# Two transformer blocks on one core: a merge placed later, a staging buffer moved, expert choice in pieces, and narrow second blocks in the 64-expert mixture

## The chip, the cores and the metric

The kernel runs on one core of a Trainium2 chip. The time is the device time of one execution in microseconds (us); less is better. Several executions are timed and their median is taken. One execution of the kernel before was recorded by the hardware profiler, and all rows below come from that one.

## What is computed

Two blocks follow each other on x of 1024 rows by 1024 numbers (float32). Of the reference only the parts that the change touches are shown:

```python
# first block, end of its attention: 16 heads of 64 columns each (yb), and a gated merge with a recurrence (ya)
merged = gates[:, :, 0] * ya + gates[:, :, 1] * yb
h = h + merged @ w_out            # then a mixture of 32 experts, 2 for each row
# second block
mix = concatenate([o, p])         # o: gated recurrence of 4 heads, p: pooling, each through its small products
h = layer_norm(ALPHA * h + mix @ w_out_2)
scores = sigmoid(h @ w_router)    # 64 experts, 8 groups of 8
# 4 best groups by the sum of their 2 best, in them the 8 best experts; their weights normed and scaled
routed[row] += weight * ((silu(h[row] @ w_gate[e]) * (h[row] @ w_up[e])) @ w_down[e])   # 8 experts e per row
out = layer_norm(ALPHA * h + routed + shared_expert(h))
```

w_gate and w_up of an expert are 1024x256, w_down is 256x1024: 3 MB in float32.

## The kernel before, in words

**Attention** (L834 ff., about 728 to 1093 us). One stream of products runs on PE over the 16 heads; a head has eight key tiles, kt 0 to 7. `beside(h, kt)` (L1067) names the work that is put beside head h at tile kt: pieces of the next head's inputs, `rec` (L975), which fetches the finished pair's rows of the recurrence's output into one tile (bufs=1) on SP, and the six parts of `merge` (L986) for a finished pair of heads pr. `MERGE` (L832) lists for each part the head from which it is due and the tile. Parts 0 and 1 multiply the attention's rows, 2 and 3 add the gated recurrence on DVE, 4 copies the rounded half to `mgh` on ACT (L999, two copies), 5 forms the remainder `mgl` on DVE (L1002, two instructions), releases the pair's buffers and sends the loads of the next pair's gates on SP (`gates`, L1009). Parts 3 and 4 both stand at kt=1, part 5 at kt=2. On the same ACT the scores of each key tile are turned to exponentials (L950), and PE's score products (L947 to L949) wait for the score buffers that these free.

**The second block's mixer** (`mixer2`, L2048). SBUF pools are stacks: a pool that is opened where another was closed waits for the readers of that memory. `mixer2` opens the pool `hc` (with `v`, the recurrence's rows) first and `hw` (weights of its input product) behind it. At its end the 4x128x128 weights of the pooling are loaded and split in tiles of `hw`; then `back` (transposes of `v` on PE, L2353) and `pool` alternate. `mixer_out2` (L2366) is next: w_out_2 comes in eight pieces of 512 KB over SP (L2388) into tiles `s0` to `s2` of a shared pool `sh`, which lie where `v` was; each piece is split by ACT (L247) and DVE (L253).

**mixer_out2's loop** goes over eight tiles t of 128 rows, in two halves of 512 columns: 48 products of 256 columns on PE, the residual on DVE (L2461), then `norm(t)` (DVE, ACT, POOL), and behind it for tile t-2 `trans` (PE, copies on ACT L2429) in half 0 and `router` (PE L2435, ACT) in half 1. At `router(3)`, in t=5, half 1, the choice of experts for the first four tiles, `route2` (L2469), is issued in one stretch: an activation on ACT and some 65 DVE instructions. The other four tiles' `route2` is issued later, in pieces, inside the mixture.

**The mixture of 64 experts** (`moe2`, L2578, and `experts`, L1382; about 2121 to 3134 us). The experts are ranked by load; rank r has room for `CAPS2[r]` rows (L2576), and a program path for overflows lies behind it. The blocks of at most 128 rows come in pairs of experts: rank 63-i whole (128 rows), rank i as 128 rows and a second block with the rest of its room. So with `CAPS2` of before pairs 0 to 3 have a second block of 96 rows, pairs 4 to 31 one of 64. The rank-i expert's weights are split in two roundings and its first block uses three products each (`mm3`, L271 to L273); the whole expert's block and the 64-row second block use plain float32 products, each of which the trace records as two. A 64-row block (`half`, L1477) puts its output on two parts of the PE columns: rows of x stand still as 64 columns, and two products with halves of the weights run on the column parts 0 and 64 (`products2`, L1481, `tile_position`).

For each block n, in this order: gather of n+3 (POOL, indirect DMA, L1569), `gate_up`, `act`, `down(n-1)` and its scatter-add, `trans(n+2)`, `h_trans(n)`, and what `todo` holds for n: one-hots (DVE) and `tabmm` (PE, L1504), which make the index tables that the gathers and scatters read, each group of blocks due four blocks ahead. The scatter-add of a block (L1691 for 128 rows, L1666 for a 64-row one) is an indirect DMA from POOL that adds to `acc_d` in DRAM; as each writes the same tensor, each waits until the one before has landed. `y`, the block's result, has two buffers, `xg`, the gathered rows, three. Weights come in thirds of 1 MB through a ring of `RAW2`=11 (L1953), and `pump` (L1425) sends the next one over SP when PE has freed its place.

Of the kernel before, what the change touches and what calls it, by code (L numbers as in the profile page):

```python
# [7 lines left out]
F32 = mybir.dt.float32  # L8
# [12 lines left out]
D = 1024  # L21
# [210 lines left out]
class Body:  # L232
# [599 lines left out]
    MERGE = (2, 0), (3, 0), (3, 0), (3, 1), (3, 1), (3, 2)  # L832

    def attention(self, rb, rk, ml):  # L834
# [4 lines left out]
        with ExitStack() as cx:  # L839
# [227 lines left out]
            def beside(h, kt):  # L1067
# [5 lines left out]
                if n < 16:  # L1073
                    if kt < 2:
                        fill += [(t_piece, n, "kq"[kt], half) for half in range(2)]
                    fill += [(m_piece, n, i, a) for i, a in
                             {3: [(7, 0), (7, 512), (6, 0)], 4: [(6, 512), (5, 0), (5, 512)],
                              5: [(4, 0), (4, 512), (3, 0)], 6: [(2, 0), (1, 0), (0, 0)]}.get(kt, ())]
                    if kt == 5:
                        fill.append((v_piece, n))  # L1080
                    if kt == 7:
                        fill += [(lambda: None,), (row_piece, n)]
                if kt == (3 if h == 15 else 4) and h > 0:
# [3 lines left out]
                for part, (late, at) in enumerate(self.MERGE):  # L1087
                    if h >= late and (h - late) % 2 == 0 and kt == at:
                        fill.append((merge, (h - late) // 2, part, 0, 2, nc.vector if part else nc.gpsimd))
# [292 lines left out]
    def experts(self, cx, blocks, xsrc, wsrc, acc_d, C, route, pre=None, fin=None, whole=lambda key: False):  # L1382
# [9 lines left out]
        N = len(blocks)  # L1392
        n0 = next(n for n, b in enumerate(blocks) if b[0] is not None)
# [8 lines left out]
        split_to = {b[2]: n for n, b in enumerate(blocks) if b[0] is None or b[3] != 64}  # L1402
# [74 lines left out]
        def half(n):  # L1477

            return blocks[n][0] is not None and blocks[n][3] == 64
# [10 lines left out]
        def onehot(n, oh=None):  # L1490
            r, off = blocks[n][:2]
            oh = ohs[n] = ep.tile([128, 8, C], BF, name="oh") if oh is None else oh
            W = 64 if half(n) else C
# [3 lines left out]
        def tabmm(n, first, a=0, b=6):  # L1497
# [3 lines left out]
            for t in range(8):  # L1501
                for h in range(2 if half(n) else 1):
                    p, kw = (slice(64 * h, 64 * h + 64), dict(tile_position=(0, 64 * h))) if half(n) else (slice(C), {})
# [4 lines left out]
        def tabfin(first, size, a=0, b=6):  # L1508
# [19 lines left out]
            for j in range(size):  # L1528
                R = blocks[first + j][3]
                idx[first + j] = (gi[:R, j:j + 1], si[:R, j:j + 1],  # L1530
                                  w[:, j:j + 1] if half(first + j) else w[:R, j:j + 1], w)
# [5 lines left out]
        while first < N1:  # L1537
            size = min((3, 2, 2, 4, 8)[min(i, 4)] if n0 else (2, 3, 4, 6, 8)[min(i, 4)], N1 - first)
            last = n0 - 2 + 2 * i if n0 and i < 2 else first - 3 if not n0 and i == 2 else \
                first - 4 if n0 or i > 2 else i - 2  # L1540
# [20 lines left out]
        def gather(n):  # L1561
# [3 lines left out]
            xg = ep.tile([128, D], F32, name="xg", bufs=3)  # L1565
# [7 lines left out]
        def trans(n):  # L1573
# [9 lines left out]
            if whole(blocks[n][2]) or half(n):  # L1583
# [11 lines left out]
        def gate_up(n, mid=None):  # L1595
            key, R = blocks[n][2:]
            ps = pg.tile([128, 512], F32, name="gups")
            if half(n):
                j = 3 * keys.index(key)
                products2(ps[:, 0:256], X.pop(n), [lambda h, w=w: w[:, :, 128 * h:128 * h + 128]  # L1600
                                                   for w in gu([raw[j], raw[j + 1]])])
# [15 lines left out]
        def act(n):  # L1617
# [3 lines left out]
            R, W = (128, 128) if half(n) else (R, 256)  # L1621
# [5 lines left out]
        def h_trans(n):  # L1627
            hh, R = Hs[n], blocks[n][3]
            ps = p1.tile([128, 2, C], F32, name="hT")
            if half(n):  # L1630
# [3 lines left out]
                ps = ps.rearrange("p (k c) -> p k c", k=2)  # L1634
            else:
# [3 lines left out]
            if whole(blocks[n][2]) or half(n):  # L1639
# [10 lines left out]
        def down(n):  # L1650
# [5 lines left out]
            if half(n):  # L1656
                ps = p1.tile([128, 1024], F32, name="yps")[:, 0:512]
                j = 3 * keys.index(key) + 2
                products2(ps, h, [lambda q, w=w: w[:, q * 512:q * 512 + 512] for w in down_(raw[j])])
                if last_of[key] == n:  # L1660
# [3 lines left out]
                nc.scalar.activation(y[:64, 0:512], ps[:64], AF.Copy, scale=w[:64])  # L1664
                nc.vector.tensor_scalar(y[:64, 512:1024], ps[64:128], w[64:128], None, op0=OP.mult)
                nc.gpsimd.indirect_dma_start(out=acc_d, out_offset=bass.IndirectOffsetOnAxis(ap=si, axis=0),  # L1666
                                             in_=y[:64], in_offset=None, compute_op=OP.add)
# [30 lines left out]
        def products(n):  # L1698
# [4 lines left out]
            gathers(n + 3)  # L1703
# [67 lines left out]
        for n in range(N):  # L1771
# [7 lines left out]
            gathers(n + 3)  # L1779
# [21 lines left out]
            if n == N1:  # L1801
                fin.load(room, lambda: ep.tile([128, D], F32, name="xg", bufs=3))
# [150 lines left out]
    RAW1, RAW2 = 13, 11  # L1953
# [94 lines left out]
    def mixer2(self, u2):  # L2048
# [317 lines left out]
    def mixer_out2(self, mo):  # L2366
# [5 lines left out]
        with ExitStack() as cx:  # L2372
# [58 lines left out]
            def router(t):  # L2431
# [16 lines left out]
            for t in range(10):  # L2448
# [4 lines left out]
                for half in range(2):  # L2453
# [122 lines left out]
    CAPS2 = [(4, 224), (28, 192), (32, 128)]  # L2576

    def moe2(self, rt):  # L2578
# [28 lines left out]
        with ExitStack() as cx:  # L2607
            tp = cx.enter_context(tc.tile_pool(reuse_waits="tile", name="rt4", bufs=1))

            def route(p1, ep):  # L2610
                late = self.route_late(Carve([ep.tile([128, D], F32, name=n, bufs=b)
                                              for n, b in (("xg", 3), ("y", 2))]))
# [143 lines left out]
```

## Time and profile before

| what | value |
|---|---|
| time, median of 3 executions | 3202.43 us (3194.46 to 3207.52) |
| time of the profiled execution | 3195.43 us |
| its span, first to last instruction | 3193.6 us |
| its mean granted PE clock | 0.961 |
| busy: PE, DVE, ACT, POOL | 92%, 57%, 39%, 20% |
| DMA | 579.71 MB, mean 182 GB/s |

PE is TensorE's products, PEld its weight loads, DVE, ACT and POOL the vector, scalar and GpSimd engines, SP the queue that sends most DMAs. In a timeline row stand the start, the duration, the engine, the line, the operation, the output and inputs, the size, and in brackets how long the engine had been idle and what ended that. Several like instructions in a row are one row (x8).

### The profile page before, as it was taken

Reading aid. Unit: us, or ns where it says so; the run is one execution under the profiler, and the core shown is the slowest. Engines: PE = TensorE matmul, PEld = TensorE weight load, DVE = VectorE, ACT = ScalarE, POOL = GpSimd, SP = SyncE. Lnnn points to the kernel's source line nnn. Section 1 sums busy time; section 2 is a strip of 40 time slices with the busy share of each in tenths; the row PEclk is TensorE's granted clock in tenths of the full one; section 3 lists DMA queues with packets and bytes.
Section 4 is the critical chain, followed back from the end, with each engine's and each line's share of the span. In section 5 each row is a group of like instructions: output and inputs, shape, how many; then the busy total and the mean of one; then the engine's idle time right before and its main releaser. Section 6 shows DMA issues by size and latency. Waiting matters only on the chain. (4 is left out here: it accounts for less than half of the span.)

```text
span 3193.6 us, 41876 instructions
## 1 busy us (share of the span) xinstructions
PE 2953.0 (92%) x15865; PEld 2183.8 (68%) x15865; DVE 1814.7 (57%) x2909; ACT 1249.6 (39%) x1929; POOL 642.9 (20%) x495
## 2 busy tenths in 40 slices
PE   5999999998999996999889998978999999999995
PEld 4778778896666893655479787955666666666663
DVE  5545651666666656566446565445655555555556
ACT  3332332444445323444343324332344444444343
POOL 0000000121000103233212232112233232333320
PEclk9999999998999997999989999979999999999997
DMA  3212120244332267999720102337899999999994
GB/s 115 66 53 86 66 73 23 97 163 110 93 93 90 92 219 275 300 330 351 239 104 28 40 18 90 132 137 242 267 282 322 303 327 313 316 316 323 314 307 144
DMA packets 225885, 579.71 MB, mean 182 GB/s; under 512 B 22421, under 2 KB 104005, under 8 KB 225653
## 3 DMA queue, kind: packets, MB, share of 16 engines
q1 hardware_dynamic: 187952, 444.37, 39.6%
q0 software_dynamic: 37296, 132.55, 16.6%
q8 instruction: 127, 2.08, 0.3%
q14 instruction: 78, 0.64, 0.1%
q10 hardware_dynamic: 432, 0.06, 0.0%
HBM read 470.22 MB, written 106.64 MB: 181 GB/s over the span
## 5 line engine op out<-in xcount | busy, mean ns | idle before, releaser
L271 PE MATMUL mm<-uh,wh 128*128 128x512 f32 x640 | 252.6, 395 | 10.8 <-ACT t L505 8.8
L273 PE MATMUL mm<-uh,wl 128*128 128x512 f32 x640 | 251.8, 393 | 0.0
L272 PE MATMUL mm<-ul,wh 128*128 128x512 f32 x640 | 251.7, 393 | 0.0
L1475 PE MATMUL gups<-raw,x 128*128 128x512 f32 (+1 forms) x536 | 236.4, 592 | 0.0
L1622 ACT ACTIVATE th<-gups 128x128 f32<-128x128 f32 (+2 forms) x136 | 49.0, 361 | 418.9 <-PE gups L1475 251.0
L1691 POOL DMA_INDIRECT acc_d<-y,si x68 | 118.3, 1740 | 438.9 <-DMA acc_d<-y,si 145.9
L1623 DVE SCALAR_TENSOR_TENSOR hh<-th,gups 128x128 f32<-128x128 f32 (+2 forms) x136 | 53.1, 390 | 241.9 <-ACT th L1622 235.7
L253 DVE TENSOR_TENSOR gl<-raw,gh 128x1024 fp32r<-128x1024 f32 x142 | 168.1, 1221 | 28.4 <-ACT gh L247 28.3
L1688 DVE TENSOR_SCALAR y<-yps,wsl 128x512 f32<-128x512 f32 (+1 forms) x95 | 71.2, 750 | 196.7 <-ACT y L1686 193.8
L271 PE MATMUL gups<-gh,xh 128*128 128x512 f32 (+1 forms) x440 | 179.8, 409 | 0.9 <-ACT xh L1589 0.9
L1686 ACT ACTIVATE y<-yps,wsl 128x512 f32<-128x512 f32 (+1 forms) x100 | 68.7, 687 | 276.9 <-PE yps L1475 146.9
L273 PE MATMUL gups<-gh,xl 128*128 128x512 f32 (+1 forms) x440 | 176.4, 401 | 0.0
L272 PE MATMUL gups<-gl,xh 128*128 128x512 f32 (+1 forms) x440 | 176.1, 400 | 0.0
L1475 PEld LDWEIGHTS gups<-raw,x 128*128 128x128 f32 (+1 forms) x536 | 95.3, 183 | 116.4 <-issue 116.4
L1579 PEld LDWEIGHTS tp<-ident,xg 128*128 128x128 f32 (+2 forms) x1088 | 114.2, 144 | 74.6 <-issue 38.5
L958 PE MATMUL o<-raw,v 128*128 128x512 f32 (+3 forms) x384 | 163.4, 514 | 0.0
L271 PEld LDWEIGHTS mm<-uh,wh 128*128 128x128 f32 x640 | 121.7, 190 | 38.1 <-ACT t L505 10.6
L247 ACT ACTIVATE gh<-raw 128x1024 fp32r<-128x1024 f32 x142 | 142.9, 1054 | 10.5 <-PE gups L273 7.7
L1579 PE MATMUL tp<-ident,xg 128*128 128x128 f32 (+2 forms) x1088 | 128.5, 262 | 15.5 <-DMA xg<-xf_d,gi 7.1
L273 PEld LDWEIGHTS mm<-uh,wl 128*128 128x128 f32 x640 | 121.6, 190 | 25.7
L272 PEld LDWEIGHTS mm<-ul,wh 128*128 128x128 f32 x640 | 121.7, 190 | 25.3
L950 ACT ACTIVATE raw<-st 128x512 f32<-128x512 f32 (+1 forms) x192 | 92.8, 490 | 117.8 <-PE st L949 116.7
(685 smaller groups left out, 7669.0 us busy)
## 6 DMA issues: line engine op xcount, KB each, us to landing
raw<-in_w_down_dram SPq DMA_DIRECT2D x69, 1024.0 KB
raw<-in_w_gate_dram SPq DMA_DIRECT2D x136, 512.0 KB
raw<-in_w_up_dram SPq DMA_DIRECT2D x136, 512.0 KB
w<-in_w_in_dram SPq DMA_DIRECT2D x20, 1024.0 KB
s<-in_w_down_dram SPq DMA_DIRECT2D x17, 1024.0 KB
s<-in_w_gate_dram SPq DMA_DIRECT2D x34, 512.0 KB
s<-in_w_up_dram SPq DMA_DIRECT2D x34, 512.0 KB
b<-in_w_gate_dram SPq DMA_DIRECT2D x22, 512.0 KB
```

Source lines behind the costliest of these rows:

```text
L247: nc.scalar.activation(hi, src, AF.Copy)
L253: e.tensor_tensor(lo, src, hi.bitcast(F32), op=OP.subtract)
L271: nc.tensor.matmul(out, lh, rh, start=start and i == 0, stop=False, **kw)
L272: nc.tensor.matmul(out, lh, rl, start=False, stop=False, **kw)
L273: nc.tensor.matmul(out, ll, rh, start=False, stop=stop and i == n - 1, **kw)
L950: nc.scalar.activation(raw[:, a - kt * 128:b - kt * 128], st, AF.Exp)
L958: nc.tensor.matmul(O[h][a // 512][:, a % 512:a % 512 + b - a], v, p[:, a - kt * 128:b - kt * 128], start=kt == 0, stop=kt == (7 if a >= 51 ...
L1475: nc.tensor.matmul(out, x, w, start=start and i == 0, stop=stop and i == len(pairs) - 1, **kw)
L1579: nc.tensor.transpose(ps[:, k // 4, (k % 4) * R:(k % 4) * R + R], xg[:R, k * 128:k * 128 + 128], self.ident[:R, :R])
L1686: nc.scalar.activation(y[:R, 0:512], ps[0][:R], AF.Copy, scale=w)
L1688: nc.vector.tensor_scalar(y[:R, 512:1024], ps[1][:R], w, None, op0=OP.mult)
L1691: nc.gpsimd.indirect_dma_start(out=acc_d, out_offset=bass.IndirectOffsetOnAxis(ap=si, axis=0), in_=y[:R], in_offset=None, compute_op=OP.add)
```

## The change

- `MERGE`: part 4 moves from tile kt=1 to kt=3, part 5 from kt=2 to kt=4; in `beside` the merge's parts are put ahead of `rec`.
- `mixer2`: the pool `hw` is opened before `hc`, so that `sh` and the other tiles of `mixer_out2` come to lie on `hw` and no longer on `v`; the pooling's weights and their two roundings take tiles of the ring `slot` (ten of 4 KB per partition).
- `mixer_out2`: `route2` of the first four tiles is advanced in pieces: three behind `norm(5)`, three behind `norm(6)`, one in t=7 after half 0; `trans(6)` comes before `norm(7)`.
- `CAPS2`: room for 224 rows (4 ranks), 192 (12), 160 (16), 128 (24) and 112 (8). So the second blocks of pairs 4 to 15 keep 64 rows, those of pairs 16 to 31 have 32 instead of 64, and the whole blocks of pairs 0 to 7 have 112 instead of 128. The number of blocks stays.
- 32-row blocks use four column parts (0, 32, 64, 96): `gate_up`, `down` and the tables with twice the products of half the columns each; the transposes of the hidden rows become two products with a picked identity on two column parts; y is scaled in four pieces of 32x256, two on ACT and two on DVE.
- Gathers run `LEAD`=5 blocks ahead instead of 3 (five `xg`), tables are due six blocks ahead instead of four; the ring of weight thirds has 10 places instead of 11. The mixture of 32 experts keeps its 3 blocks.

```diff
-    MERGE = (2, 0), (3, 0), (3, 0), (3, 1), (3, 1), (3, 2)
+    MERGE = (2, 0), (3, 0), (3, 0), (3, 1), (3, 3), (3, 4)
...
+            wp = cx.enter_context(tc.tile_pool(reuse_waits="tile", name="hw", bufs=2))
             c1 = cx.enter_context(tc.tile_pool(reuse_waits="tile", name="hc", bufs=1))
-            wp = cx.enter_context(tc.tile_pool(reuse_waits="tile", name="hw", bufs=2))
...
-                wpl = wp.tile([128, 4, 128], F32, name="w")
+                wpl = slot()[:, :512].rearrange("p (g d) -> p g d", g=4)
                 nc.sync.dma_start(wpl, IN["w_pool_2"][0].rearrange("g c d -> c g d"))
-                wplh = wp.tile([128, 4, 128], F32R, name="wh")
-                wpll = wp.tile([128, 4, 128], F32R, name="wl")
+                wplh, wpll = [z[:, a] for z in [slot(F32R).rearrange("p (a g d) -> p a g d", a=2, g=4)] for a in range(2)]
...
-                if t == 3:
-                    for _ in self.route2(rtp, lg[0], bias, 0, 4):
-                        pass
+            first = self.route2(rtp, lg[0], bias, 0, 4)
+
+            def advance(n):
+                for _ in range(n):
+                    next(first, None)
...
-                    if t > 1:
+                    if t > 1 and (half or t != 8):
                         (router if half else trans)(t - 2)
+                    if t == 7 and not half:
+                        advance(1)
+                if t == 7:
+                    trans(6)
                 if t < 8:
                     norm(t)
                     loadx(t + 2)
+                    advance({5: 3, 6: 3}.get(t, 0))
...
-    CAPS2 = [(4, 224), (28, 192), (32, 128)]
+    CAPS2 = [(4, 224), (12, 192), (16, 160), (24, 128), (8, 112)]
...
+        LEAD = 5 if blocks[0][0] is None else 3
...
-        def products2(ps, xs, ws):
-
+        def narrow(n):
+
+
+            return 128 // blocks[n][3] if blocks[n][0] is not None and blocks[n][3] in (32, 64) else 0
+
+        def products2(G, ps, xs, ws):
+
+            R = 128 // G
             for i, (x, w) in enumerate(zip(xs, ws)):
-                for h in range(2):
-                    nc.tensor.matmul(ps[64 * h:64 * h + 64], x, w(h), start=i == 0, stop=i == len(xs) - 1,
-                                     skip_group_check=True, tile_position=(0, 64 * h))
+                for h in range(G):
+                    nc.tensor.matmul(ps[R * h:R * h + R], x, w(h), start=i == 0, stop=i == len(xs) - 1,
+                                     skip_group_check=True, tile_position=(0, R * h))
...
+            elif narrow(n):
+
+                ps = ps[:, 0, :64].rearrange("p (k c) -> p k c", k=2)
+                v = self.ident.rearrange("p (k a c) -> p a k c", k=2, a=2)
+                for a in range(2):
+                    nc.tensor.matmul(ps[64 * a:64 * a + 64], hh[:, 0:64], v[:, a], start=True, stop=True,
+                                     skip_group_check=True, tile_position=(0, 64 * a))
...
-                nc.scalar.activation(y[:64, 0:512], ps[:64], AF.Copy, scale=w[:64])
-                nc.vector.tensor_scalar(y[:64, 512:1024], ps[64:128], w[64:128], None, op0=OP.mult)
+                for q in range(G):
+                    p, c = slice(R * q, R * q + R), slice(W * q, W * q + W)
+                    if q < G // 2:
+                        nc.scalar.activation(y[:R, c], ps[p], AF.Copy, scale=w[p])
+                    else:
+                        nc.vector.tensor_scalar(y[:R, c], ps[p], w[p], None, op0=OP.mult)
...
-            gathers(n + 3)
+            gathers(n + LEAD)
...
-    RAW1, RAW2 = 13, 11
+    RAW1, RAW2 = 13, 10
```

## Rows read from the trace of the kernel before

**Rows 1.** The page's first two parts: PE's busy time; granted clock in 40 slices.

```profile
PE 2953.0 (92%) x15865; PEld 2183.8 (68%) x15865; DVE 1814.7 (57%) x2909; ACT 1249.6 (39%) x1929; POOL 642.9 (20%) x495
...
PEclk9999999998999997999989999979999999999997
```

**Rows 2.** Windows: length, busy PE PEld DVE ACT POOL, granted clock, DMA share, GB/s.

```profile
819.00:861.00 42.00, 39.43 (x192) 28.46 (x191) 27.95 (x60) 21.16 (x45) 2.35 (x1) 0.95 0.32 88
...
2075.80:2125.00 49.20, 31.43 (x195) 30.18 (x195) 22.53 (x51) 21.10 (x24) 8.81 (x10) 0.71 0.28 100
2400.00:3100.00 700.00, 697.51 (x3929) 432.64 (x3926) 395.57 (x552) 297.92 (x449) 214.64 (x148) 1.00 1.00 317
1300.00:1350.00 50.00, 50.00 (x260) 30.37 (x259) 32.61 (x46) 24.37 (x36) 17.85 (x10) 1.00 1.03 349
```

**Rows 3.** Timeline, 901 to 903 us: a pair's merge beside head 7's attention.

```profile
901.02 1.15 ACT L999 ACTIVATE mgh<-rec 128x512 fp32r<-128x512 f32 x2 [2.30 <-DVE rec L996]
901.68 1.29 DVE L1002 SCALAR_TENSOR_TENSOR mgl<-rec,mgh 128x512 fp32r<-128x512 f32 x2 [0.70 <-ACT mgh L999]
...
902.49 0.50 PE L947 MATMUL st<-kq 105*128 105x512 f32 x1 [2.57 <-ACT raw L950]
```

**Rows 4.** Waits of PE, 800 to 1035 us: us in total, times, longest.

```profile
PE st L947 <- ACT raw L950: 15.4, 6, 2.6
```

**Rows 5.** Timeline, 1967 to 2008 us: from mixer2 into mixer_out2.

```profile
1967.34 1.04 PE L2353 MATMUL tp<-ident,v 128*128 128x128 f32 x8
...
1968.51 13.89 SPq L2388 DMA_DIRECT2D s<-in_w_out_dram  x8
...
1973.08 0.54 PE L271 MATMUL mm<-woh,mxh 128*128 128x256 f32 x1 [3.31 <-DVE mxl L263]
...
1982.18 1.06 ACT L247 ACTIVATE woh<-s 128x1024 fp32r<-128x1024 f32 x1 [6.21 <-DMA s<-in_w_out_dram]
...
1983.29 0.51 PE L271 MATMUL mm<-woh,mxh 128*128 128x256 f32 x1 [3.30 <-ACT woh L247]
...
1995.85 0.69 DVE L2461 SCALAR_TENSOR_TENSOR xr<-xr,mm 128x512 f32<-128x512 f32 x1 [3.31 <-PE mm L273]
...
2007.37 0.69 DVE L2461 SCALAR_TENSOR_TENSOR xr<-xr,mm 128x512 f32<-128x512 f32 x1 [2.54 <-PE mm L273]
```

**Rows 6.** Timeline, 2067 to 2090 us: first and last instruction of route2, PE behind it.

```profile
2067.68 0.29 DVE L2476 TENSOR_SCALAR sc<-sc 128x256 f32<-128x256 f32 x1 [5.15 <-ACT sc L2475]
...
2080.06 0.29 DVE L2517 CAST ex<-W 128x256 bf16<-128x256 f32 x1
...
2086.17 3.67 PE L2435 MATMUL tp<-rw,xT 128*128 128x64 f32 x16 [10.32 <-ACT xT L2429]
```

**Rows 7.** Timeline of PE, 2384 to 2416 us: one pair of experts and the next's start.

```profile
2384.17 3.67 PE L1485 MATMUL gups<-raw,x 128*64 128x256 f32 x32
...
2391.89 7.03 PE L1475 MATMUL gups<-raw,x 128*128 128x512 f32 x16
2398.85 1.94 PE L1485 MATMUL yps<-raw,hT 128*64 128x512 f32 x8
...
2401.35 0.42 PE L1504 MATMUL tab<-cols,oh 128*64 128x6 bf16 x16
...
2412.40 3.67 PE L1485 MATMUL gups<-raw,x 128*64 128x256 f32 x32
```

**Rows 8.** Timeline of POOL, 2595 to 2626 us: scatter-adds three apart.

```profile
2595.39 1.57 POOL L1691 DMA_INDIRECT acc_d<-y,si  x1 [8.04 <-DVE gl L253]
...
2623.33 1.56 POOL L1691 DMA_INDIRECT acc_d<-y,si  x1 [7.64 <-DVE gl L253]
```

**Rows 9.** Instructions of L1691 (128-row scatter-adds), 2400 to 3100 us: landing.

```profile
DMA to landing us min/median/max: 6.2/9.1/12.0
```

**Rows 10.** Instructions of L1666 (64-row scatter-adds), 2400 to 3100 us: landing.

```profile
DMA to landing us min/median/max: 5.6/7.4/10.2
```

**Rows 11.** Waits of PE, 2400 to 3100 us.

```profile
PE tp L1579 <- DMA xg<-h_d,gi: 2.5, 2, 1.4
```

More of the change, by code (lines that the diff above doesn't have):

```diff
@@ L1082, in beside @@
                         fill += [(lambda: None,), (row_piece, n)]
+                for part, (late, at) in enumerate(self.MERGE):
+                    if h >= late and (h - late) % 2 == 0 and kt == at:
+                        fill.append((merge, (h - late) // 2, part, 0, 2, nc.vector if part else nc.gpsimd))
                 if kt == (3 if h == 15 else 4) and h > 0:
@@ L1400, in experts @@
         last_of = {b[2]: n for n, b in enumerate(blocks)}
-        split_to = {b[2]: n for n, b in enumerate(blocks) if b[0] is None or b[3] != 64}
+        split_to = {b[2]: n for n, b in enumerate(blocks) if b[0] is None or b[3] not in (32, 64)}
         Wt = {}
@@ L1501, in tabmm @@
             for t in range(8):
-                for h in range(2 if half(n) else 1):
-                    p, kw = (slice(64 * h, 64 * h + 64), dict(tile_position=(0, 64 * h))) if half(n) else (slice(C), {})
+                R = 128 // (narrow(n) or 1)
+                for h in range(narrow(n) or 1):
+                    p, kw = (slice(R * h, R * h + R), dict(tile_position=(0, R * h))) if narrow(n) else (slice(C), {})
                     nc.tensor.matmul(tab[0][p, n - first, a:b], oh[:, t, :p.stop - (p.start or 0)],
@@ L1530, in tabfin @@
                 idx[first + j] = (gi[:R, j:j + 1], si[:R, j:j + 1],
-                                  w[:, j:j + 1] if half(first + j) else w[:R, j:j + 1], w)
+                                  w[:, j:j + 1] if narrow(first + j) else w[:R, j:j + 1], w)
         todo = {}
@@ L1539, in experts @@
             last = n0 - 2 + 2 * i if n0 and i < 2 else first - 3 if not n0 and i == 2 else \
-                first - 4 if n0 or i > 2 else i - 2
+                first - (LEAD + 1 if i > 2 else 4) if n0 or i > 2 else i - 2
             for j in range(size if i > 1 or n0 and i else 0):
@@ L1564, in gather @@
             r, t, _, R = blocks[n]
-            xg = ep.tile([128, D], F32, name="xg", bufs=3)
+            xg = ep.tile([128, D], F32, name="xg", bufs=LEAD)
             if r is None:
@@ L1582, in trans @@
             v = lambda z: z.rearrange("p (a k) c -> p a k c", a=2)
-            if whole(blocks[n][2]) or half(n):
+            if whole(blocks[n][2]) or narrow(n):
                 x = ep.tile([128, 8, C], F32, name="x", tag="xh")[:, :, :R]
@@ L1597, in gate_up @@
             ps = pg.tile([128, 512], F32, name="gups")
[L1598 to L1601, printed above, removed]
+            if G := narrow(n):
+                j, W = 3 * keys.index(key), 256 // G
+                products2(G, ps[:, 0:2 * W], X.pop(n), [lambda h, w=w: w[:, :, W * h:W * h + W]
+                                                        for w in gu([raw[j], raw[j + 1]])])
                 Hs[n] = ps
@@ L1629, in h_trans @@
             ps = p1.tile([128, 2, C], F32, name="hT")
-            if half(n):
+            if narrow(n) == 2:
                 ps = ps[:, 0, :128]
@@ L1638, in h_trans @@
                     nc.tensor.transpose(ps[:, k], hh[:R, k * 128:k * 128 + 128], self.ident[:R, :R])
-            if whole(blocks[n][2]) or half(n):
+            if whole(blocks[n][2]) or narrow(n):
                 h = ep.tile([128, 2, C], F32, name="hT", tag="hTh")[:, :, :R]
@@ L1655, in down @@
                 pass
-            if half(n):
-                ps = p1.tile([128, 1024], F32, name="yps")[:, 0:512]
+            if G := narrow(n):
+                W = 1024 // G
+                ps = p1.tile([128, 1024], F32, name="yps")[:, 0:W]
                 j = 3 * keys.index(key) + 2
-                products2(ps, h, [lambda q, w=w: w[:, q * 512:q * 512 + 512] for w in down_(raw[j])])
+                products2(G, ps, h, [lambda q, w=w: w[:, q * W:q * W + W] for w in down_(raw[j])])
                 if last_of[key] == n:
@@ L1778, in experts @@
                     Wt[key] = gu([raw[3 * ki], raw[3 * ki + 1]]), down_(raw[3 * ki + 2])
-            gathers(n + 3)
+            gathers(n + (LEAD if n >= n0 + 2 else 3))
             if n == n0 - 1:
@@ L1801, in experts @@
             if n == N1:
-                fin.load(room, lambda: ep.tile([128, D], F32, name="xg", bufs=3))
+                fin.load(room, lambda: ep.tile([128, D], F32, name="xg", bufs=LEAD))
             if n >= n0:
```

13 lines of the change are left out of this document (4 added, 9 removed).

## The prediction

> **What bounds the kernel now.** I read the page first: PE is busy 92% of the span, and the clock slices fall below 9 only in a few places [rows 1]. So time is to be had from products, from places where PE stands still, and from what the lower clock costs behind these. Then the windows, one for each place that the change touches [rows 2]: in the attention window of 42 us PE is busy 39.43 us at clock 0.95; at the end of the second mixer's output stage 31.43 of 49.2 us at 0.71; in the second mixture 697.51 of 700 us at 1.00. The mixture is then a row of products with hardly a gap, at 317 GB/s; the first mixture's window shows 349 GB/s, so the DMA engines can give more than the second asks. Last the timelines of the four places, taken in turn.
>
> My sum is made against the profiled execution, 3195.43 us. The median of the three runs is 3202.43, 7.0 above it; I add 7.0 at the end.
>
> **Part A, the merge.** Six times PE waits 2.57 us for ACT's exponentials [rows 4]. The timeline of one of them [rows 3] shows why: ACT stood still for 2.30 us on the pair's `rec` from DVE, because part 4 is queued ahead of the exponentials, then spent 1.15 us on it; PE's score product came 2.57 us late. ACT's shift of 3.45 us thus cost PE 2.57 us: 0.9 us is absorbed. Behind the stall the clock falls: 0.95 over 42 us is 42 x 0.05 = 2.1 us of full-clock work, at most all of it lost time, at least none. I take 1.4, since PE is busy for 94% of that window and seldom has slack to hide it. An event costs 2.57 + 1.4 = 4.0 us. Two tiles later part 3 is long done, so ACT's wait goes, but the 1.15 us of copies stay, now at kt=3, and the 1.29 us of part 5 on DVE at kt=4, behind which `rec` and the gate loads are queued on SP and DVE. By the absorbed 0.9 us the copies leave 0.25; I take 0.4 left of each event, with 0 and 2.4 (1.15 + 1.29, nothing hidden) as ends. Net 3.6 x 6 = **21 us** (from 6 x (2.57 - 2.4) = 1 to 6 x 4.7 = 28; the lower end needs both shifts to hit PE in full, so I use 10 to 24 for the range). The merge ahead of `rec` costs nothing for heads below 15, where both stand at kt=4 in the other order; for head 15 `rec` finds its one buffer held until part 5 at kt=4, one tile later, with four tiles of products as cover.
>
> **Part B, the staging of w_out_2.** SP sends all eight pieces from 1968.51 on for 13.89 us, just behind the last transposes of `v` at 1967.34 [rows 5]: their tiles lie on `v`. ACT waits 6.21 us for a piece, PE 3.30 us at 1983.29, and tile 0 ends at 1995.85, tile 1 at 2007.37, so a tile takes 11.5 us. PE's first product at 1973.08 waits for the mixer's own last split on DVE, which stays. With the pieces already there, as `hw` is free once the in-projection's weights are used, tile 0 would run from 1973.1 for 11.5 us, plus the price of the low clock behind that 3.31 us gap: between 0 and 11.5 (the whole tile at the lower of the two levels, 1.2 of 2.4 GHz); in part A it was at most 2.1 behind 2.57, so 2.1 x 3.31 / 2.57 = 2.7 here. Tile 0 then ends at 1987.3, 8.5 us earlier. Against it stand the slot for the pooling's weights, free only when an earlier split from that ring is done, and the splits of w_out_2 that now share ACT and DVE with the mixer's last ones; the nearest row for either is one 1.06 us split [rows 5], so I take 2 us off for the two, and get **6.5 us** (0, if they delay the mixer's end by as much; 11 without clock loss or waits).
>
> **Part C, expert choice in pieces.** `route2` holds DVE from 2067.68 to 2080.35 [rows 6]; `norm(5)` waits behind it, and PE then stands still for 10.32 us before `router(5)`'s product. With the pieces behind `norm(5)` and `norm(6)`, that gap goes. What goes with it: of the 31.43 busy us at clock 0.71 [rows 2] at most 0.29 x 31.43 = 9.1 us are lost to the clock, by three gaps, so 3 us are this one's. At most 13.3. But the same 12.7 us of DVE now lie among the last three norms, where DVE, 22.53 of 49.2 us busy, becomes the pace; `trans(6)`'s copies now stand ahead of `norm(7)` on ACT, about 1 us. I take **9 us** (0, if the pieces stretch the last three tiles by as much).
>
> **Part D, the 32-row blocks.** A pair of experts takes PE 28.23 us, from 2384.17 to 2412.40 [rows 7]. Of it the 64-row block has 3.67 us of `gate_up` in 32 records. The whole block's 16 records of 512 columns take 7.03, so 256 columns are 0.22; 16 such streams are 3.51, and the halves run two abreast with 0.005 us per record on top. On four parts, 64 records of 128 columns are 16 x 0.11 + 64 x 0.005 = 2.1: 1.6 less. `down` has 1.94 for 8 records where 4 x 0.44 = 1.76 are streams, 0.02 on top for each; 16 records four abreast are 0.88 + 0.2 to 0.36 = 1.1: 0.8 less. The tables' 16 small products take 0.42; 32 add 0.35; the two plain products for the transpose add some 0.1. Net PE saves 2.0 per pair, for pairs 16 to 31: 16 x 2.0 = 32 us, if PE alone counts.
>
> It doesn't. Three scatter-adds of a pair follow each other, each waiting for the landing of the one before: 2623.33 - 2595.39 = 27.94 us for three [rows 8], where the median landings are 9.1, 9.1 and 7.4 [rows 9, 10], 25.6 together; the other 2.3 us are three restarts. So this chain is as long as PE's period, within 0.3 us. With 32 rows I let a landing shorten by as much per row as from 128 to 64: 1.7 / 64 x 32 = 0.85, to 6.6 us; the chain becomes 27.1 us, 1.1 below the period of now. `y` has two buffers, so PE can't run ahead of the chain for long. I take 1.1 x 16 = **17.6 us**; ends 0 (the landing doesn't shorten) and 32 to 35 (the chain doesn't hold PE, down to its shortest landings). The 112-row blocks lie in pairs 0 to 7, where PE's 28.2 us stay: nothing. Four pieces of y instead of two put one more small instruction on ACT and one on DVE, both under 60% busy in the stretch: nothing.
>
> The Trainium skill speaks against four parts, in "TensorE: Matmul & The Clock Gate", "Part 3: Packing small matmuls": a weight load overlaps running products only where its row group differs, and all column parts share theirs. By it part D would give nothing, as 64 loads replace 32. The 0.005 us per record worked out above, on two parts of one row group, speak against it; whether they do on four, no row shows.
>
> **LEAD, RAW2.** PE waits 2.5 us in 700 for gathered rows [rows 11]; with five blocks' lead I count **2 us** for the mixture (0 to 4). One place less in the ring of weights costs nothing: at 27.1 instead of 28.2 us per pair the mixture asks for 317 x 28.2 / 27.1 = 330 GB/s, and 349 were given elsewhere [rows 2]. Were that cover gone, a place is 28.23 / 6 = 4.7 us of lead, lost once.
>
> Sum: 21 + 6.5 + 9 + 17.6 + 2 = 56 us; 3195.4 - 56 = 3139, and 7 more: **3146 us**.
>
> **The rivals.**
> - *PE alone sets the mixture's period.* For it: 697.51 busy of 700. Against it: the chain's 27.94. Then part D gives 32: 3132 us. Chance 0.17.
> - *Part D gives nothing*, because products on four parts cost as much as on two (from 3.67 / 64 = 0.057 us per record on), or because a landing doesn't depend on rows so low. 3195.4 - 38.5 + 7 = 3164 us. For it: nothing in these rows shows four parts or a 32-row landing. Against it: two parts run abreast, and 64 rows land sooner than 128. Chance 0.23.
> - *The stalls of A to C come back elsewhere*: part 4's copies and part 5 hit PE in full, SP's pieces delay the mixer's end, the pieces of `route2` stretch the last tiles. About 10 us of 36 are left: 3172 us. Chance 0.12.
> - *Slower: the scatter chain grows.* Gathers five blocks ahead share POOL's queue and the DMA engines with the scatter-adds. With A, B, C and LEAD at 38.5, the kernel is slower by 16 only if the mixture's 16 narrow pairs lose 54 us, 3.4 each: a mean landing of 9.7 us instead of 8.5. The longest rows are 12.0 and 10.2 [rows 9, 10]; with all at these a pair takes 36.5 us, 8.3 more, and the kernel 3202 - 38 + 133 = 3297. From 1.1 us more per landing it decides. Against it: there are fewer rows to move. Chance 0.05.
>
> The forecast has 0.43.
>
> **How the numbers follow.** A measurement of this kernel can tell about 0.5%, 16 us, from no change: faster is below 3186, slower above 3218. The forecast and the first two rivals are faster but for a few hundredths, the third in two of three cases: 0.43 + 0.17 + 0.22 + 0.08, less what I can't see, gives 0.87; same 0.08, slower 0.05. The range goes down to the first rival with A to C near their ends, 3195 - 24 - 11 - 13 - 32 - 2 + 7 = 3120, less 4 for LEAD's end and the shortest landings, 3114; and up to the third rival with its own doubt, 3180.
>
> **What would show it.** Right: the six waits of PE on L950 gone and clock 1.00 in those windows; SP's L2388 sent before the last L2353, and tile 0's last L2461 near 1988 minus A's gain; no gap above 5 us ahead of L2435; PE's pairs 16 to 31 at 27.1 us with `gate_up` of 32-row blocks at 2.1 us in 64 records; PE's waits now for `yps` or `y` behind the scatter-adds. Wrong: PE's period at 26.2 (PE alone), at 28.2 (part D gives nothing), or 32-row scatter-adds that land in 7.4 us or more.

## The result, and the profile after

The changed kernel takes 3161.27 us (median of 4, 3157.68 to 3166.06) where the kernel before takes 3201.61 (median of 4 in the same comparison): a ratio of 0.9876, 95% interval 0.9852 to 0.99, or 40 us less. The forecast was 3146 us, 56 less, with a range of 3114 to 3180. The profiled execution has a span of 3159.9 us, 33.7 less than the span of before; stages are compared between these two.

The page after, its first two parts; against [rows 1] PE's busy time is 45 us less at the same share:

```profile
PE 2907.6 (92%) x16809; PEld 2163.2 (68%) x16809; DVE 1815.4 (57%) x2925; ACT 1248.5 (40%) x1945; POOL 636.7 (20%) x497
...
PEclk9999999998999997999999999988999999999997
```

Windows after, columns as in [rows 2]: attention beside a merge, the end of the second mixer's output, the mixture's opening, the stretch of 32-row blocks:

```profile
790.00:832.00 42.00, 41.73 (x218) 31.16 (x216) 29.71 (x62) 24.08 (x50) 3.95 (x2) 1.00 0.31 89
...
2056.00:2105.00 49.00, 31.20 (x165) 23.95 (x165) 32.96 (x127) 18.05 (x23) 8.84 (x15) 0.70 0.31 108
2180.00:2203.00 23.00, 15.36 (x100) 11.01 (x100) 15.52 (x40) 3.32 (x7) 6.81 (x5) 0.75 0.95 318
2668.00:3060.00 392.00, 367.28 (x3034) 238.20 (x3034) 217.10 (x320) 166.64 (x267) 120.44 (x84) 1.00 0.98 310
```

The attention window is now full, at clock 1.00. The end of the output stage looks like before: 31.20 busy of 49 at 0.70. And in the mixture, where PE had been busy 697.51 of 700 us, it now stands still twice: for a third of the opening's window, and for 25 of 392 us in the 32-row stretch.

Where the 33.7 us come from, by the start of like instructions in the two traces: the output product behind attention ends 24.4 us earlier (A); the in-projection of the second mixer ends 22.8 us earlier, as the first mixture, which the change leaves alone, took 2.9 us more and the mixer 1.2 less; tile 0 of its output ends 29.8 us earlier (B, 7.0); the second mixture's first product starts 36.9 us earlier (C, 7.1); its last product comes 33.7 us earlier. So the mixture, which was to give 19.6 us, **lost 3.2**: from its first product to the first `gate_up` of a 64-row block (its opening) it took 9.6 us more, 239.3 instead of 229.7, and from pair 16 on 6.4 less.

Waits of PE after, 776 to 1011 us. The only group listed stands for 1.3 us; the waits of [rows 4] are gone:

```profile
PE tm L929 <- DVE mz L925: 1.3, 5, 0.3
```

Timeline after, from mixer2 into mixer_out2, against [rows 5]:

```profile
1933.16 22.07 SPq L2405 DMA_DIRECT2D s<-in_w_out_dram  x8
...
1939.04 0.80 PE L271 MATMUL mm<-slot 128*128 128x512 f32 x1 [2.47 <-ACT slot L247]
...
1951.19 0.39 PE L271 MATMUL mm<-woh,mxh 128*128 128x256 f32 x1 [2.15 <-ACT woh L247]
...
1966.04 0.69 DVE L2481 SCALAR_TENSOR_TENSOR xr<-xr,mm 128x512 f32<-128x512 f32 x1 [3.77 <-PE mm L273]
```

SP begins to send w_out_2 18 us before the first output product, no longer behind the last transposes. The wait for the pooling's slot is there, 2.47 where 1.06 us stood before, and it costs 0.9 us up to the output's first product. The 3.30 us wait in the middle of tile 0 is gone.

Timeline of PE after, the end of the output stage, against [rows 6]: a gap of 11.83 us, now behind DVE and ahead of `trans(7)`.

```profile
2078.97 1.94 PE L2445 MATMUL tp<-ident,xf 128*128 128x128 f32 x8 [11.83 <-DVE xf L2433]
```

Timeline of PE after, 32-row blocks, against [rows 7]:

```profile
2676.49 0.34 PE L1645 MATMUL hT<-ident,hh 128*64 128x64 f32 x4 [1.37 <-DVE hh L1629]
...
2683.82 1.07 PE L1489 MATMUL yps<-raw,hT 128*32 128x256 f32 x16
...
2695.86 0.36 PE L1509 MATMUL tab<-cols,oh 128*32 128x6 bf16 x32
...
2696.52 1.95 PE L1489 MATMUL gups<-raw,x 128*32 128x128 f32 x64
...
3057.56 1.96 PE L1489 MATMUL gups<-raw,x 128*32 128x128 f32 x64
```

`gate_up` has 1.95 us for 64 records (forecast 2.1), `down` 1.07 (1.1), the tables 0.36 for 32 records (0.8). The last two rows are 13 pairs apart: (3057.56 - 2696.52) / 13 = 27.8 us a pair, where PE's own work is 26.2 by the run `two_acc` below. Single pairs take from 26.3 to 29.5 us. Waits of PE (the longest group) and of ACT in that stretch, and the landings of its 32-row and 128-row scatter-adds (against [rows 9, 10]):

```profile
PE hT L1645 <- DVE hh L1629: 14.1, 14, 1.4
```

```profile
ACT y L1703 <- DMA acc_d<-y,si: 97.1, 24, 6.2
```

```profile
DMA to landing us min/median/max: 4.8/7.0/7.2
```

```profile
DMA to landing us min/median/max: 7.1/9.7/11.6
```

ACT, which writes y, waits 97.1 us for scatter-adds to land and leave a buffer of y free. PE's own waits are for `hh` and y; that they come from the scatter-adds is shown only by `two_acc` below. The landings are thin evidence: the trace has them for 4 of the 14 32-row scatter-adds and 6 of the 28 128-row ones.

Timeline after in the mixture's opening: four one-hots on DVE, 4.62 us in a row, and PE's tables wait for each, 5.1 us in all (waits of PE, 2089 to 2328 us); the kernel before has no such wait there.

```profile
2197.54 4.62 DVE L1498 TENSOR_TENSOR oh<-slot_r,pos 128x1024 bf16<-128x1024 f16 x4
```

```profile
2198.81 0.38 PE L1509 MATMUL tab<-cols,oh 128*128 128x6 bf16 x8 [2.80 <-DVE oh L1498]
```

```profile
PE tab L1509 <- DVE oh L1498: 5.1, 4, 2.8
```

### The profile page after: what moved, and what is told of

It reads as the page before. It is cut to its first block, busy times and chain, and to the rows that moved or that the text cites. A ratio compares the mean times of both kernels' runs of the same rounds, so it can differ in the third digit from the quotient of the medians.

```text
span 3159.9 us, 43800 instructions
## 1 busy us (share of the span) xinstructions
PE 2907.6 (92%) x16809; PEld 2163.2 (68%) x16809; DVE 1815.4 (57%) x2925; ACT 1248.5 (40%) x1945; POOL 636.7 (20%) x497
## 5 line engine op out<-in xcount | busy, mean ns | idle before, releaser
L1477 PE MATMUL gups<-raw,x 128*128 128x512 f32 (+2 forms) x528 | 234.1, 595 | 0.0
L1705 DVE TENSOR_SCALAR y<-yps,wsl 128x512 f32<-128x512 f32 (+2 forms) x95 | 71.2, 750 | 232.1 <-ACT y L1703 228.6
L1627 ACT ACTIVATE th<-gups 128x64 f32<-128x64 f32 (+3 forms) x136 | 48.3, 355 | 394.9 <-PE gups L1477 240.8
L1703 ACT ACTIVATE y<-yps,wsl 128x512 f32<-128x512 f32 (+2 forms) x100 | 68.7, 687 | 307.5 <-DMA acc_d<-y,si 104.3
L1628 DVE SCALAR_TENSOR_TENSOR hh<-th,gups 128x64 f32<-128x64 f32 (+3 forms) x136 | 52.1, 383 | 222.6 <-ACT th L1627 222.4
L253 DVE TENSOR_TENSOR gl<-raw,gh 128x1024 fp32r<-128x1024 f32 x136 | 161.2, 1220 | 29.0 <-ACT gh L247 27.3
L1477 PEld LDWEIGHTS gups<-raw,x 128*128 128x128 f32 (+2 forms) x528 | 92.1, 180 | 114.9 <-issue 114.1
L1584 PEld LDWEIGHTS tp<-ident,xg 128*128 128x128 f32 (+4 forms) x1088 | 113.6, 144 | 67.4 <-issue 36.4
L958 PE MATMUL o<-raw,v 128*128 128x512 f32 (+3 forms) x384 | 156.4, 495 | 0.0
L1584 PE MATMUL tp<-ident,xg 128*128 128x128 f32 (+4 forms) x1088 | 127.0, 260 | 15.2 <-DMA xg<-xf_d,gi 8.3
L1477 PE MATMUL yps<-raw,hT 128*128 128x512 f32 (+2 forms) x296 | 133.0, 592 | 1.4 <-ACT hT L1653 1.4
```

Source lines behind the costliest of these rows:

```text
L253: e.tensor_tensor(lo, src, hi.bitcast(F32), op=OP.subtract)
L958: nc.tensor.matmul(O[h][a // 512][:, a % 512:a % 512 + b - a], v, p[:, a - kt * 128:b - kt * 128], start=kt == 0, stop=kt == (7 if a >= 51 ...
L1477: nc.tensor.matmul(out, x, w, start=start and i == 0, stop=stop and i == len(pairs) - 1, **kw)
L1584: nc.tensor.transpose(ps[:, k // 4, (k % 4) * R:(k % 4) * R + R], xg[:R, k * 128:k * 128 + 128], self.ident[:R, :R])
L1628: nc.vector.scalar_tensor_tensor(hh[:R, :W], th[:R, :W], 1.0, ps[:R, 0:W], op0=OP.add, op1=OP.mult)
L1703: nc.scalar.activation(y[:R, 0:512], ps[0][:R], AF.Copy, scale=w)
```

## The experiments

Most of these kernels have one execution. The first mixture, which no edit touches, takes from 391.2 to 396.5 us in the fourteen traces, and the changed kernel's four times lie 8.4 us apart; so a difference of a few us is taken from the stage that the edit touches.

**One part alone, or one undone.** `a_alone` is the kernel before with part A; `b_undone` and `c_undone` are the changed kernel without B or C.

```diff
-    MERGE = (2, 0), (3, 0), (3, 0), (3, 1), (3, 1), (3, 2)
+    MERGE = (2, 0), (3, 0), (3, 0), (3, 1), (3, 3), (3, 4)
```

> The kernel before with part A alone (merge parts 4 and 5 at tiles 3 and 4, merge ahead of rec). Theory, A is worth what the stage shows: the six waits of 2.57 us are gone, attention ends 25 to 26 us earlier than in the kernel before, and the execution's time is 3195 - 24 = 3171 us. Rival, the stages behind attention give part of it back (the first mixture shows 2.8 us less than attention's lead in the changed kernel): 3175 us or more.

Measured: 3173.74 us in one execution (kernel before on that chip 3199.0), 25 less, and the six waits are gone. In the traces attention ends 27.7 us earlier than before, and the span is 21.7 us shorter. A is worth 22 to 28 us by this; whether the stages behind it give back a part, as the rival has it, one execution between the two forecasts cannot tell.

> The changed kernel with mixer2's pools in the old order and the pooling's weights in their own tiles again. Theory, part B is worth 7 us (from the in-projection's last product to the end of tile 0 it takes 30.6 us now and 37.6 before): 3161 + 7 = 3168 us, with SP's loads of w_out_2 behind the last transposes of v again. Rival, what tile 0 gains is lost again at the expert choice, where DVE paces: 3162 us.

Measured: 3166.67 us in one execution, 5.4 above the changed kernel. SP's loads are late again:

```profile
1944.09 13.59 SPq L2406 DMA_DIRECT2D s<-in_w_out_dram  x8
```

From the in-projection's end to the mixture's first product it takes 159.7 us instead of 153.9: B is worth 5.7 there. The rival's loss at the expert choice doesn't show.

> The changed kernel with route2 of the first four tiles in one stretch at router(3) and trans(6) where it was. Theory, part C is worth what the two traces differ by between the end of tile 5's second half and the mixture's first product, 7 us: 3167 us, with the 10.3 us gap ahead of router(5) back. Rival, the gap of 11.8 us that now stands ahead of trans(7) replaces it in full and C is worth nothing: 3160 us.

Measured: 3168.1 us in one execution, 6.8 above; the same stretch takes 161.2 us, 7.3 more. The old gap is back at its place, and a second one of 5.28 us behind it:

```profile
2059.26 1.97 PE L2452 MATMUL tp<-rw,xT 128*128 128x64 f32 x8 [10.29 <-ACT xT L2446]
```

So C gains 7 us although the largest gap only moved: it removed two gaps, 10.3 and 5.3 us, and made one of 11.8. The gaps are the smaller part of it. Windows from the last residual of tile 5 to the mixture's first product, before and after, columns as in [rows 2]:

```profile
2061.84:2126.28 64.44, 46.67 (x320) 45.27 (x319) 30.77 (x116) 27.61 (x30) 8.81 (x10) 0.77 0.30 107
...
2031.85:2089.35 57.50, 42.57 (x321) 41.44 (x319) 35.60 (x116) 28.05 (x30) 10.44 (x15) 0.79 0.35 127
```

PE stands still for 14.9 us instead of 17.8, 2.8 less, and is busy for 4.1 us less with as many products. One place shows it: the 16 products of a router took 3.67 us behind the 10.32 us gap [rows 6] and take 2.81 behind one of 1.69:

```profile
2064.32 2.81 PE L2452 MATMUL tp<-rw,xT 128*128 128x64 f32 x16 [1.69 <-ACT xT L2446]
```

The gap of 11.8 us was put to the test by holding back the last pieces:

```diff
-                    if t == 7 and not half:
-                        advance(1)
...
-                    advance({5: 3, 6: 3}.get(t, 0))
+                    advance({5: 3, 6: 1, 7: 3}.get(t, 0))
```

> The changed kernel with only one piece of route2 behind norm(6) and the last three behind norm(7). Theory, the 11.8 us gap of PE ahead of trans(7) is DVE's pace: the pieces stand ahead of the last residual and norm(7), which then comes some 5 us sooner, and the mixture starts 4 to 6 us sooner: 3156 us. Rival, the pieces are needed by the mixture's opening and only move behind: 3161 us.

Measured: 3149.65 us in one execution; the stretch takes 148.3 us, 5.7 less, and the gap is halved:

```profile
2071.60 1.73 PE L2445 MATMUL tp<-ident,xf 128*128 128x128 f32 x7 [5.96 <-DVE gv L2524]
```

The stage bears out the theory: DVE's pieces stood ahead of norm(7). The other half of the 11.6 us lies in stages that this edit doesn't touch: 1.7 ahead of the in-projection's end, 4.2 in the mixture, behind an opening as long as the changed kernel's.

**The chain of landings.** `two_acc` lets scatter-adds alternate between two tensors; results in the second one are left out of the output.

```diff
-                nc.gpsimd.indirect_dma_start(out=acc_d, ...
+                nc.gpsimd.indirect_dma_start(out=self.acc2_d if n0 and n > n0 and n % 2 else acc_d, ...
```

> The changed kernel, scatter-adds alternate between two accumulators, so that a scatter-add waits for the landing of the one before the last. The second accumulator is zeroed ahead of the mixture and not added to the output: every second block's result is left out of it. Theory, the chain of landings sets the pace of the 32-row pairs (27.9 us): they go to PE's own 26.2 us, 16 x 1.5 = 24 us less, 3136 us; 64-row pairs stay at 28.2. Rival, the DMA engines' throughput sets it (busy share 0.97, 308 GB/s): landings grow longer as more lie in flight, pairs stay at 27.9 us, 3160 us.

Measured: 3134.53 us in one execution, 26.7 less; by the traces all of it lies in the mixture. The window, two of its `gate_up`s twelve pairs apart, and the landings of 32-row and 128-row scatter-adds:

```profile
2668.00:3060.00 392.00, 387.48 (x3126) 253.16 (x3128) 232.74 (x342) 184.28 (x289) 123.44 (x86) 1.00 0.99 327
```

```profile
2694.43 1.96 PE L1489 MATMUL gups<-raw,x 128*32 128x128 f32 x64
...
3008.39 1.95 PE L1489 MATMUL gups<-s,x 128*32 128x128 f32 x64
```

```profile
DMA to landing us min/median/max: 6.5/7.4/8.2
```

```profile
DMA to landing us min/median/max: 9.2/10.3/12.2
```

(3008.39 - 2694.43) / 12 = 26.2 us a pair: PE's own time. The landings are no shorter than with one accumulator, and it no longer matters. The DMA engines' busy share had been 0.98 at 310 GB/s and is 0.99 at 327: the share near 1 was no limit. What set the pace was that each scatter-add waits for the one before.

**What the 32-row blocks give.** `caps_old` has the ranks' room of the kernel before.

```diff
-    CAPS2 = [(4, 224), (12, 192), (16, 160), (24, 128), (8, 112)]
+    CAPS2 = [(4, 224), (28, 192), (32, 128)]
```

> The changed kernel with the ranks' room of the kernel before, so that second blocks have 64 rows again and whole blocks 128; all else as changed. Theory, the chain of landings paces the 32-row pairs at 27.9 us where PE alone paces 64-row pairs at 28.2: the 32-row blocks are worth 16 x 0.35 = 6 us, and without them 3161 + 6 = 3167 us. Rival, fewer rows shorten the chain as forecast, by 1.1 us a pair, and something else took it: 3178 us.

Measured: 3167.33 us in one execution, 6.1 above; by the traces the mixture is 4.9 us longer and ten pairs from pair 16 on take 28.3 us each, with no wait of PE listed from 2668 to 3060 us. The 32-row blocks give 5 to 6 us of the 17.6 forecast.

This trace has all 14 landings of 64-row scatter-adds from 2668 to 3060 us, and the one of `opening` (below) has all 14 of 32-row ones. 64 rows:

```profile
DMA to landing us min/median/max: 4.8/6.9/9.0
```

32 rows:

```profile
DMA to landing us min/median/max: 5.7/7.0/8.3
```

So in these traces a landing does not get shorter from 64 rows to 32. The 7.4 us of [rows 10] come from six landings.

**Buffers of y.** `y3` has three for y, and gathers four blocks ahead.

```diff
-        LEAD = 5 if blocks[0][0] is None else 3
+        LEAD = 4 if blocks[0][0] is None else 3
...
-                y = ep.tile([128, 1024], F32, name="y")
+                y = ep.tile([128, 1024], F32, name="y", bufs=3 if n0 else 2)
```

> The changed kernel with three buffers for y and gathers four blocks ahead (the same memory). Theory, the pace is the sum of the landings, and a third buffer only lets PE run further ahead once: 32-row pairs stay at 27.9 us, 3161 us, within 5. Rival, two buffers tie PE to each single landing: pairs at 26.5 us or so, 3161 - 16 x 1.3 = 3140 us. Either way four blocks of lead cost less than three did.

Measured: 3153.66 us in one execution. Pairs take 27.6 us (14 from 2690.4 to 3076.5), not 26.5: the third buffer doesn't lift the chain. A scatter-add starts 0.77 us (median) behind the landing before it, as in the changed kernel. PE's wait has changed its name, with one block of lead less; a third buffer with five blocks of lead was not tried:

```profile
PE tp L1584 <- DMA xg<-h_d,gi: 21.5, 11, 3.6
```

Of the 8 us that its span is shorter, 4.1 lie in the 32-row stretch (14 pairs by 0.3) and 3.9 ahead of the mixture, where the edit does nothing. `c_undone` and `c_later`, whose 32-row stretch is the changed kernel's, differ from it there by 0.2 us a pair, so the 0.3 is hardly more than that.

**Lead and tables.** `lead3` takes both back to the values of before, in the changed kernel; `opening` only keeps the first tables at four blocks.

```diff
-        LEAD = 5 if blocks[0][0] is None else 3
+        LEAD = 3
...
-                first - (LEAD + 1 if i > 2 else 4) if n0 or i > 2 else i - 2
+                first - 4 if n0 or i > 2 else i - 2
```

> The changed kernel with gathers three blocks ahead again, tables due four blocks ahead, three xg buffers; ring of 10 and 32-row blocks stay. Theory, the earlier tables cost the mixture's opening: from the gate_up that follows the shared blocks to the third one after it 31.6 us now and 24.9 before; this comes back, 6 to 9 us less, 3153 us. Rival 1, the opening waits for expert choice and not for the order of the tables: 3161 us. Rival 2, gathers come late without the lead: narrow pairs above 28.2 us, 3165 us or more.

Measured: 3170.84 us (median of 4), ratio to the kernel before 0.9908 (0.9885 to 0.9931), 9.6 above the changed kernel. Half the theory held: the opening's passage takes 23.7 us. But the 32-row stretch pays more than that, with 29.2 us a pair, by the second rival's mechanism. Waits of PE, 2668 to 3090 us:

```profile
PE tp L1584 <- DMA xg<-h_d,gi: 33.1, 18, 3.9
```

Gathers are queued on POOL behind a scatter-add that waits, so a late chain makes late gathers; before, PE waited 2.5 us for them [rows 11]. Two rows of POOL in `lead3`:

```profile
2722.49 1.70 POOL L1708 DMA_INDIRECT acc_d<-y,si  x1 [5.78 <-DMA acc_d<-y,si]
2724.49 0.90 POOL L1574 DMA_INDIRECT xg<-h_d,gi  x1 [0.30 <-issue]
```

```diff
-                first - (LEAD + 1 if i > 2 else 4) if n0 or i > 2 else i - 2
+                first - (LEAD + 1 if i > 4 else 4) if n0 or i > 2 else i - 2
```

> The changed kernel with tables due six blocks ahead only from the sixth group of tables on, four blocks ahead before that. Theory, the opening of the mixture takes 24 us as with three blocks of lead instead of 32, and the 32-row pairs stay at 27.9 with few waits for gathers: 8 us less, 3153 us. Rival, the tables that were early in the opening come late in the next stretch: 3160 us.

Measured: 3152.85 us (median of 4), ratio 0.9847 (0.9831 to 0.9864), 8.4 below the changed kernel. The opening's passage takes 25.0 us, and PE's waits for one-hots are gone from it. Its window is full, but for half a microsecond, at a higher clock:

```profile
2180.00:2203.00 23.00, 22.51 (x110) 16.48 (x110) 15.16 (x39) 6.19 (x9) 5.76 (x5) 0.87 0.93 303
```

`opening` and `lead3` differ by 18 us: with 32-row blocks that is what five blocks of lead, with the later tables that go with it, are worth.

**Versions that beat both.** `two_full` is `opening` with two accumulators, whose sum is made when the last stage loads its rows.

> Two accumulators as before, now complete: the rows of the second one are added by DMAs when the last stage loads its rows, so nothing is left out; and the tables' due times in the opening as in the run of that name. Theory, 32-row pairs at 26.7 us (27 us less by the run without the sum), 8 us in the opening, 6 to 13 us more at the end for 4 MB of adding: 3161 - 27 - 8 + 10 = 3136 us. Rival, adding DMAs are slow and stand one after the other ahead of the last normalisation: 3155 us or more.

Measured: 3143.16 us (median of 4), ratio 0.9823 (0.9806 to 0.9839). The sum cost 14 us at the end; each adding DMA waited for a load:

```profile
3083.57 0.85 POOL L69 DMA_DIRECT2D raw<-acc_d  x1 [2.51 <-DMA raw<-acc_d]
3087.39 0.84 POOL L69 DMA_DIRECT2D raw<-acc_d  x1 [2.97 <-DMA raw<-acc_d]
```

```diff
-            nc.sync.dma_start(H[t], self.o.acc_d[t * 128:t * 128 + 128])
-            nc.gpsimd.dma_start(H[t], self.o.acc2_d[t * 128:t * 128 + 128], accum_op=OP.add)
+            nc.sync.dma_start(H[t], self.o.acc2_d[t * 128:t * 128 + 128])
+        for t in range(8):
+            nc.gpsimd.dma_start(H[t], self.o.acc_d[t * 128:t * 128 + 128], accum_op=OP.add)
```

> Two accumulators, complete, opening as in the run of that name; the second accumulator takes no result of the last two blocks, so that the last stage loads its rows from it at once, and the first one's rows are then added by DMAs back to back. Theory, the 14 us that the sum cost at the end were the adding DMAs waiting one after the other for a load each: 8 to 10 us less than with loads first, 3134 us. Rival, the adding itself takes the time: 3143 us.

Measured: 3132.72 us in one execution. By the traces the sum costs 5 us at the end, 8 less than in `two_full`, with the adding DMAs sent back to back (the diff above is against `two_full` and leaves out the edit to the scatter-adds):

```profile
3075.56 5.22 POOL L70 DMA_DIRECT2D raw<-acc_d  x6 [0.27 <-issue]
```

> The last two edits together on the changed kernel: two accumulators with the quick end and the opening's tables (3133 us by one look), and the last pieces of route2 behind norm(7) (11 us less by one look). Theory, they touch different stages and add up: 3133 - 10 = 3123 us, ratio to the kernel before 0.975. Rival, the late pieces hold DVE in the opening, where the tables now come later: 3130 us.

Measured: 3130.1 us (median of 4), ratio 0.9786 (0.9755 to 0.9817), the shortest of all. The 32-row stretch keeps its pace, but from the in-projection's end to the mixture's first product it takes 151.3 us, 3 more than in `c_later`. These 3 us stand ahead of the end of tile 0, which no late piece and no table reaches (34.2 us from the in-projection's end, 31.2 in `c_later`). From tile 5's last residual to the mixture's first product both take 51.2 to 51.3 us, and the opening takes 232.7 us where `two_end` has 233.1. So the stages add up, and the rival, whose number came out, does not show in its stage. The 10 us that the forecast took from `c_later` were too many: 5.7 of its 11.6 lay in the stage. Where the 3 us come from was not tried.

## Why the prediction held, and where it was off

The time lies in the range because A, B and C came out at 38.5 us of 36.5. The mixture's share did not: 19.6 us were forecast, and 3.2 were lost. The measured 3161 is nearer to the second rival's 3164 than to 3146; that the total held although the mixture's terms did not is in part luck.

**A, 21 us forecast:** 24.4 in the trace, 25 alone by the times; in the thirteen traces that have A, attention ends 23.0 to 27.7 us earlier. Mechanism and size were right; the order of merge and `rec` was not tried by itself; of each event nothing like the 0.4 us allowed was left in PE's waits.

**B, 6.5:** 7.0 by the traces, 5.7 when undone. The 2 us put down for slot and splits were 0.9.

**C, 9:** 7.1 and 7.3. "DVE becomes the pace" was right, and it showed as a new gap of 11.8 us, larger than the one removed. My bound missed that the old kernel had a second gap, 5.3 us, to remove. Of the 13.3 us at most, the 10.3 of the gap came to 2.8 over all gaps, since the new one takes the rest back, and the 3 us for the clock to 4.1 of PE's busy time, if the clock is what shortened it.

**D, 17.6:** 5 to 6. The step that failed is "with 32 rows I let a landing shorten by as much per row as from 128 to 64": 32 rows land in 7.0 us, not 6.6, and where all landings are known 64 rows land in 6.9. The 128-row landings beside them did not fall either (9.1 before [rows 9], 9.7 after; 10.0 in `caps_old`). The chain's period, by the pairs, is 27.8 us, not 27.1. With no shortening the prediction's own rows give a chain of 27.94 against PE's 28.23, 16 x 0.3 = 5 us, so its lower end of 0 was too low, too. That the chain and not PE would decide was right, and the first rival (PE alone, 3132) is excluded by 27.8 against 26.2; with the chain cut, its 26.2 us a pair came out as worked out. Of the second rival, the first cause (four parts cost as much as two) is excluded; its other cause, that a landing doesn't depend on rows so low, is borne out. The Trainium skill's rule in "TensorE: Matmul & The Clock Gate", "Part 3: Packing small matmuls", is that a weight load overlaps running products only where its row group differs; the section also names a load to the background weight buffer as one that is pulled ahead. The first, taken alone, does not agree with the trace, where all four parts share the rows; which buffer a load takes, no run here shows. Instructions of L1489 after, 2668 to 3060 us, loads ahead of `gate_up`, and the timeline of the loads of one `gate_up`:

```profile
L1489 PEld LDWEIGHTS gups<-raw,x x672: 106/110/110, 2669.4 to 3059.1; 128*32 128x32 f32 x168
```

```profile
2696.52 1.69 PEld L1489 LDWEIGHTS gups<-raw,x 128*32 128x32 f32 x64 [0.17 <-issue]
```

64 loads of 0.110 us are 7.0 us, but they lie within 1.69, and the whole `gate_up` takes 1.95; so the loads overlap each other and the products.

**LEAD, 2:** this term had the wrong sign for the opening and was far too small behind it. I priced what the lead gains by a wait that the kernel before had, 2.5 us, when PE was as slow as the chain, and did not price the tables that the lead moves: one-hots of 1.15 us each on DVE now stand ahead of PE's products in the opening. By the traces the opening took 9.6 us more than before, and 6.0 of these came back with the first tables put back (8.4 by the times). Once PE is faster than the chain, the lead with its tables is worth 18.

**RAW2, 0:** among PE's waits in the mixture after, 2089 to 3090 us, none is for weights.

Sum: 24.4 - 2.9 + 1.2 + 7.0 + 7.1 - 3.2 = 33.6 us, the span's 33.7 but for rounding. The 2.9 us of the first mixture are no waits: those for gathers grew by 1.1 us (7.1 to 8.3 in all), another shrank by 1.9. With 395.4 us it lies among the 391.2 to 396.5 of the fourteen traces, where before has 392.6; so nothing shows that the 2.9 belong to the change.

## What to carry to other kernels

A rule of thumb for a chain of dependent DMAs: compare its period with the engine's before making the engine faster; where they are within a few per cent, as 27.9 and 28.2 us here, only what shortens or cuts the chain counts. Two accumulators cut it, at the price of one sum, and that price depends on what the adding waits for. And a lead is paid in the stage where it is built up: move the work that it needs only where the engines that do it have room.

## What the runs showed of the hardware that was not expected

- A busy share of the DMA engines of 0.98 did not mean that they were full: with the chain cut they moved 327 instead of 310 GB/s at 0.99.
- A scatter-add's landing doesn't depend on its rows when they are few: 7.0 us for 32 rows (`opening`), 6.9 for 64 (`caps_old`); 128 rows took 9.5 and 10.0 there. With two accumulators the shortest 128-row landing was 9.2 us, where it is 6.2 in these two.
- Four column parts run close to their streams: 64 records of 128 columns take 1.95 us, 0.03 us each, where 16 streams of 128 columns at the rate of [rows 7] are 1.76.
